# Products that nobody reads in TensorE's waits, and two modulation groups traced at another place

## The chip, the cores and the metric

The kernel runs on one core of a Trainium2 chip, in one launch. A core has five engines that run beside each other, each with its own queue in order: TensorE (PE in the profile; PEld is its weight load), VectorE (DVE), ScalarE (ACT), GpSimd (POOL) and SyncE (SP), which here only issues DMA transfers. ScalarE and GpSimd issue transfers too, from their own queues. TensorE writes to PSUM, eight banks of 128 x 512 f32. The metric is the device time of one execution in microseconds; lower is better.

## The reference, cut to what matters

The program is a hybrid layer on 256 tokens of 1024 channels, followed by a second block of two layers (differential and latent attention, a stick-breaking attention, two cross attentions, two MLPs), which the change does not touch. All data are f32. Of the first layer this matters here:

```python
mod = silu(c) @ ada_w + ada_b                    # 1024 x 6144
sh1, sc1, g1, sh2, sc2, g2 = split(mod, 6)
h = rms_norm(x, norm1_g) * (1 + sc1) + sh1       # first norm
z = h @ w_in                                     # q k v, index, rwkv (zr), two gates
attn = dsa_sparse_attention(...)                 # index scores, top 64, softmax
rw = rwkv7_branch(zr, ...)                       # a recurrence over the tokens
x = x + g1 * ((sigmoid(ga) * (attn @ w_attn_br) + sigmoid(gr) * (rw @ w_rwkv_br)) @ w_out)
h2 = rms_norm(x, norm2_g) * (1 + sc2) + sh2
x = x + g2 * moe_ffn(h2, ...)                    # router, top 8 of 64 experts, shared expert
```

The modulation has 6144 columns; the kernel makes them in three groups of 2048 (g = 0, 1, 2). Group 0 is sh1 and sc1, group 1 is g1 and sh2, group 2 is sc2 and g2. In `moe_ffn`, sigmoid scores choose 8 experts of 64 for each token, by groups; `sh_gate`, `sh_up` and `sh_down` are the shared expert, which all tokens use.

## The kernel before, in words

**Precision.** Most dense products are made of three products of split operands: `split_into` (L152, L153) writes a high part on ScalarE and the low rest on VectorE, and `mm3` (L186 to L188) adds high x high, high x low and low x high into one bank. Weights come in tiles of 128 x 2048 through SyncE's queue (`wload`, L142), from a ring of buffers, and are split in blocks of 1024 columns into three buffers. Transposes, the modulation and the experts' products are plain f32; a plain f32 product counts as two TensorE instructions in the trace.

**Order.** The program is traced in Python; a planner then sets the order of each engine's queue. An instruction that is traced earlier ranks higher; the planner goes through time by its own estimates of durations and gives each engine the highest-ranking instruction whose operands it holds to be there. So later work fills gaps of earlier work. On the chip each queue is strictly in that order: if an operand comes later than planned, the engine stands. `later(n)` lowers the rank of a block by n places. `after(engine)` sets what its block traces on that engine behind the last instruction traced there before; this is an order in the queue, not a wait.

**First norm.** `modulation(K, 0, ...)` (L965) multiplies the columns of silu(c) with eight blocks of ada_w, four products a block, into the bank "mod"; VectorE adds ada_b (L969). `first_h` meanwhile scales x and transposes it: `turn` (L1011) makes four transposes into a bank, three times ahead of the modulation's columns and once more behind them. `mod_cols` (L980) transposes the sum; from it come the scale s1 and the shift b1 (L1017, L1018). Then f = s * x + b (L1025, L1027) is split into hTh and hTl. `zr_in` makes the first projection products from it with `dense_T` (L186 to L188, tile hTh): a weight block of 1024 columns serves 24 products.

**Recurrence and modulation.** Behind `zr_in`, `first_mixer` traces modulation groups 1 and 2 and `router_in` with `later(400)`, behind ScalarE's last instruction at that place, and then `rwkv(K, zs, rwT, 0)`, the first half of the heads (four of eight). Each group has eight loads of 1 MB into one buffer "adaw" (SyncE's queue, L963), 32 products, a load of ada_b (ScalarE's queue, L952), the sum on VectorE (L969) and a store of the row to DRAM (ScalarE's queue, L972). The bank "mod" exists once, so group 2's first product needs group 1's sum to be done. `router_in` transposes the columns of groups 1 and 2, loads the router's weight and two small tensors on ScalarE's queue and one on GpSimd's, and makes eight products. The half of the recurrence is a chain of small products (L1082 to L1321) with VectorE and ScalarE between them; its last activation on ScalarE is the split of its result (L152, w<-rw). Behind it come the projections of the attention, the index scores and the choice (`dsa_choose`, L1367 to L1376, L1382), the second half of the recurrence, `dsa`, and the gates' projections.

**Routing.** `Moe.start` transposes the logits (L1655), finishes the shared expert's gate products, makes the row of norms (`row`, four products on TensorE at L295, a copy on VectorE at L298), and traces `hidden` (L1688 to L1693: copies, two products with the row on VectorE, a silu), `route` (VectorE, L1711 to L1752: sigmoid scores, the maxima by groups, the selection `selb` at L1737; three products with it on TensorE at L1741 to L1743; positions `pos` and gate weights `gw`) and `plan` (experts ordered by their number of tokens). `shared_in(K, "sh_up", up)` is a generator: the first `next` makes the products of the first half of the weight, the second those of the rest. `take` gathers the first experts' tokens: one-hot matrices P (L1873) and 32 products (L1887), which ScalarE and VectorE copy out of PSUM (L1894, L1892). The shared expert's down weight is split with the subtraction on GpSimd (L153 on POOL).

**Experts.** 64 experts in 26 units; each expert's three weights of 1 MB come through SyncE's queue (L1930, L1933) into the ring as buffers come free. The first ones are loaded ahead, until the ring is full.

## Time and profile before

| what | us |
|---|---|
| runs of the kernel before | 1696.97, 1698.87, 1699.32 |
| their median | 1698.87 |
| the profiled execution, its own time | 1700.63 |
| its span, first to last instruction | 1698.70 |
| TensorE busy | 1615.2 (95% of the span) |
| VectorE busy | 832.5 (49%) |
| ScalarE busy | 677.6 (40%) |
| GpSimd busy | 84.7 (5%) |
| mean granted clock of TensorE | 0.981 |

How the views are read. In the **stretches**, a line is a piece of time from the span's start: from:to and its length, then the busy time of PE, PEld, DVE, ACT and POOL, each with its count of instructions, then the mean granted clock of TensorE (1.00 is 2.4 GHz, 0.50 is 1.2 GHz), the busy share of the 16 DMA engines and GB/s. In the **timeline**, a line has the start, the length, the engine, the line of the kernel, the operation, out<-in by the program's names, the shape, and how many instructions were merged; in brackets stands how long the engine had been idle before, and what ended that. Successive products overlap, so the step from one start to the next is what a product costs, not its length. SPq and ACTq are the instructions that issue transfers. In the **list of transfers** a line has the count, the size of one and the median time from issue to landing; in the **view of one tile** a line has the shortest, median and longest duration in ns, and when the first and the last one began.

### The profile page before, as it was taken

What the parts mean: (1) busy time and instruction counts of PE and PEld (TensorE: products, weight loads), DVE (VectorE), ACT (ScalarE), POOL (GpSimd) and SP (SyncE); (2) the same over time, 40 slices, a digit from 0 to 9 for tenths busy, and PEclk for the clock granted to TensorE, in tenths of its full rate; (3) what the DMA queues carried; (4) which work ended last, traced back from release to release, by engine and by line L of the source; (5) the groups of instructions that cost most, each with busy time, mean ns of one, the idle gap of its engine ahead of it and who ended that gap; (6) DMA issues with size and microseconds to landing.
All of it is one profiled execution on the core that took longest, in us unless ns stands there. A gap on an engine that the chain in (4) does not pass through costs nothing. (4 is left out here: it accounts for less than half of the span.)

```text
span 1698.7 us, 28945 instructions
## 1 busy us (share of the span) xinstructions
PE 1615.2 (95%) x11894; PEld 1230.2 (72%) x11894; DVE 832.5 (49%) x1538; ACT 677.6 (40%) x1141; POOL 84.7 (5%) x105
## 2 busy tenths in 40 slices
PE   6999999997989999999999999999999999999997
PEld 3967667885547565546665587889998876989996
DVE  3664786676211311211211446666555677665554
ACT  3432444553122122122122546655444455554443
POOL 2000000103000000000000111211000000000000
PEclk8999899998999999999999999999999999999999
DMA  9555641874999999999999652546555533445551
GB/s 376 154 173 171 214 153 45 298 272 163 414 416 412 380 395 413 415 412 412 378 415 412 226 172 94 191 154 208 187 185 198 175 115 110 149 162 198 182 190 50
DMA packets 137942, 417.76 MB, mean 246 GB/s; under 512 B 10666, under 2 KB 17588, under 8 KB 118352
## 3 DMA queue, kind: packets, MB, share of 16 engines
q1 hardware_dynamic: 125872, 394.81, 62.3%
q0 software_dynamic: 4336, 12.34, 2.2%
q10 hardware_dynamic: 7600, 8.74, 1.8%
q8 instruction: 94, 1.54, 0.4%
q14 instruction: 40, 0.33, 0.1%
HBM read 409.57 MB, written 6.32 MB: 245 GB/s over the span
## 5 line engine op out<-in xcount | busy, mean ns | idle before, releaser
L153 DVE TENSOR_TENSOR w<-w 128x1024 fp32r<-128x1024 f32 (+1 forms) x283 | 347.6, 1230 | 259.0 <-ACT w L152 258.2
L152 ACT ACTIVATE w<-w 128x1024 fp32r<-128x1024 f32 (+1 forms) x285 | 299.9, 1054 | 317.6 <-PE acc L188 226.6
L1947 PE MATMUL tmp<-w 128*32 128x256 f32 (+2 forms) x2560 | 200.8, 393 | 10.2 <-DMA w<-in_exp_up_dram 8.6
L1947 PEld LDWEIGHTS tmp<-w 128*32 128x32 f32 (+2 forms) x2560 | 120.0, 121 | 81.9 <-issue 12.5
L188 PE MATMUL acc<-hTh,w 128*128 128x256 f32 (+2 forms) x552 | 159.0, 289 | 0.4 <-DVE w L153 0.4
L187 PE MATMUL acc<-hTl,w 128*128 128x256 f32 (+2 forms) x552 | 159.1, 288 | 0.0
L186 PE MATMUL acc<-hTh,w 128*128 128x256 f32 (+2 forms) x552 | 158.1, 287 | 0.7 <-ACT hTh L152 0.7
L186 PE MATMUL tmp<-hTh,w 128*128 128x256 f32 x512 | 143.3, 280 | 0.0
L188 PE MATMUL tmp<-hTh,w 128*128 128x256 f32 x512 | 142.9, 279 | 0.0
L187 PE MATMUL tmp<-hTl,w 128*128 128x256 f32 x512 | 142.9, 279 | 0.0
L188 PEld LDWEIGHTS acc<-hTh,w 128*128 128x128 f32 (+1 forms) x552 | 105.3, 191 | 5.5 <-issue 4.3
L187 PEld LDWEIGHTS acc<-hTl,w 128*128 128x128 f32 (+1 forms) x552 | 105.7, 192 | 4.3 <-issue 3.5
L1975 PE MATMUL tmp<-w,fT 128*32 128x512 f32 (+2 forms) x640 | 108.1, 598 | 0.5 <-ACT fT L1963 0.5
L186 PEld LDWEIGHTS acc<-hTh,w 128*128 128x128 f32 (+1 forms) x552 | 105.8, 192 | 3.3 <-issue 2.0
L186 PE MATMUL acc<-w,gh 128*128 128x512 f32 x256 | 99.9, 390 | 0.0
L188 PE MATMUL acc<-w,gl 128*128 128x512 f32 x256 | 99.8, 390 | 0.0
L187 PE MATMUL acc<-w,gh 128*128 128x512 f32 x256 | 99.7, 389 | 0.0
L186 PEld LDWEIGHTS tmp<-hTh,w 128*128 128x128 f32 x512 | 96.1, 188 | 0.5
L188 PEld LDWEIGHTS tmp<-hTh,w 128*128 128x128 f32 x512 | 96.2, 188 | 0.1
L187 PEld LDWEIGHTS tmp<-hTl,w 128*128 128x128 f32 x512 | 95.9, 187 | 0.5
L1951 ACT ACTIVATE fs<-tmp 128x256 f32<-128x256 f32 x26 | 10.0, 384 | 214.0 <-PE tmp L1947 214.0
L1953 DVE SCALAR_TENSOR_TENSOR ff<-tmp,gsl,fs 128x256 f32<-128x256 f32 x26 | 12.6, 484 | 167.4 <-ACT fs L1951 167.4
(633 smaller groups left out, 2913.0 us busy)
## 6 DMA issues: line engine op xcount, KB each, us to landing
w<-in_exp_gate_dram SPq DMA_DIRECT2D x64, 1024.0 KB, 15.7
w<-in_exp_up_dram SPq DMA_DIRECT2D x64, 1024.0 KB, 18.2
w<-in_exp_down_dram SPq DMA_DIRECT2D x64, 1024.0 KB, 14.8
w<-in_mlp_w_dram SPq DMA_DIRECT2D x64, 1024.0 KB, 5.2
w<-in_w_in_dram SPq DMA_DIRECT2D x23, 1024.0 KB, 6.0
adaw<-in_ada_w_dram SPq DMA_DIRECT2D x16, 1024.0 KB, 4.9
w<-in_xa_wkv_dram SPq DMA_DIRECT2D x16, 1024.0 KB, 12.7
w<-in_sb_w_in_dram SPq DMA_DIRECT2D x12, 1024.0 KB, 5.2
```

What stands on the lines that cost most here:

```text
L152: self.nc.scalar.activation(hi, src, AF.Copy)
L153: self.sub.tensor_tensor(lo, src, hi.bitcast(F32), op=OP.subtract)
L186: mm(out, lh, rh, start=first, stop=False, skip_group_check=True)
L187: mm(out, lh, rl, start=False, stop=False, skip_group_check=True)
L188: mm(out, ll, rh, start=False, stop=last, skip_group_check=True)
L1947: nc.tensor.matmul(b[at:at + w, x * 256:x * 256 + 256], X[:, k, i * 128 + at:i * 128 + at + w], d[n][:, k], start=(x == 0 and k == 0), sto ...
L1951: nc.scalar.activation(s, b[:, 0:256], AF.Silu)
L1953: nc.vector.scalar_tensor_tensor(f, b[:, 256:512], g, s, op0=OP.mult, op1=OP.mult)
L1975: nc.tensor.matmul(b[at:at + w], fT[:, k, at:at + w], d["exp_down"][:, k, n * 512:n * 512 + 512], start=(k == 0), stop=(k == 1), skip_grou ...
```

## The change

A new method `idle` makes n products of the identity with 512 columns of X (f32) into a bank that is not read, behind TensorE's last traced instruction. It is called three times: one product behind modulation group 0, three behind the last transposes of the first norm, five in `Moe.start`. There the second half of the sh_up products is traced directly behind the first, ahead of the five, of the row of norms and of `route`, and no longer behind `take`. In `first_mixer`, groups 1 and 2 and `router_in` are traced behind the first half of the recurrence, inside the scope "dsa", without `later(400)`; the block stands behind ScalarE's last instruction of the recurrence's half.

```diff
+    def idle(self, n, x, tag):
+
+        with self.after(self.PE):
+            b = self.bank(tag)
+            for _ in range(n):
+                self.nc.tensor.matmul(b, self.ident, x, start=True, stop=True, skip_group_check=True)
...
         if k < 7:
             yield
+    if g == 0:
+        K.idle(1, K.X[:, 0, :512], "acc")
     nc.vector.tensor_add(mb, b, mb)
...
             b = banks[k // 2] if k < 6 else turn(6, "tmp")
+            if k == 6:
+                K.idle(3, K.X[:, 0, :512], "acc")
             f = K.t([128, 2, T], "fhT", 2)
...
         adap = K.open("ada")
-        with K.later(400), K.after(K.ACT):
-            for g in (1, 2):
-                for _ in modulation(K, g, first, adap):
-                    pass
-            with K.stream(pool=first, tmp="mod"):
-                router_in(K, first)
         with K.scope("dsa"):
             with K.scope("rwkv0"):
                 rwkv(K, zs, rwT, 0)
+            with K.after(K.ACT):
+                for g in (1, 2):
+                    for _ in modulation(K, g, first, adap):
+                        pass
+                with K.stream(pool=first, tmp="mod"):
+                    router_in(K, first)
...
         rest = shared_in(K, "sh_up", up)
         next(rest)
+        next(rest, None)
+        K.idle(5, K.X[:, 0, :512], "mod")
         row = nm.row()
         s = K.t([128, 2, T], "shs")
         self.hidden(K.gate, s, row, True)
...
         self.take("S", {"S": 0}, tags=("tmp", "tmp", "acc"))
         next(plan, None)
-        next(rest, None)
         self.hidden(up, s, row, False)
```

## Rows read from the trace of the kernel before

**Rows 1.** Stretches: first projection, routing, experts; busy of five engines, clock, DMA.
```profile
42.50:85.00 42.50, 42.09 (x338) 38.81 (x337) 27.01 (x46) 20.57 (x30) 1.54 (x3) 1.00 0.50 154
...
395.00:405.00 10.00, 8.40 (x45) 7.05 (x44) 7.13 (x33) 4.30 (x7) 1.75 (x2) 0.61 0.00 1
...
600.00:700.00 100.00, 97.29 (x749) 59.29 (x748) 18.99 (x41) 23.89 (x43) 2.16 (x4) 1.00 1.00 405
```

**Rows 2.** Stretches between changes of the granted clock; its number is third from the end.
```profile
23.98:27.39 3.41, 2.81 (x29) 1.28 (x25) 0.00 (x0) 0.00 (x0) 0.00 (x0) 1.00 1.00 399
...
30.80:37.63 6.83, 5.84 (x25) 5.51 (x26) 6.71 (x10) 5.58 (x10) 3.01 (x6) 0.50 1.05 384
...
184.40:194.64 10.24, 8.07 (x33) 4.86 (x34) 4.79 (x12) 5.89 (x11) 0.00 (x0) 0.50 0.61 215
...
392.60:396.00 3.40, 0.40 (x6) 0.30 (x6) 3.12 (x22) 1.11 (x4) 0.00 (x0) 0.50 0.01 2
...
399.45:402.86 3.41, 3.37 (x16) 3.08 (x15) 1.18 (x10) 1.78 (x4) 0.00 (x0) 0.50 0.01 2
```

**Rows 3.** Timeline of TensorE at the first norm and the first projection products.
```profile
28.72 0.66 PE L980 MATMUL tmp<-ident,modr 128*128 128x128 f32 x4 [0.81 <-DVE modr L969]
29.80 0.63 PE L1011 MATMUL tmp<-ident,xs 128*128 128x128 f32 x4 [0.42 <-DVE b L1018]
...
32.08 0.80 PE L186 MATMUL acc<-hTh,w 128*128 128x256 f32 x2 [0.69 <-ACT hTh L152]
...
33.18 0.42 PE L188 MATMUL acc<-hTh,w 128*128 128x256 f32 x1
...
37.45 0.36 PE L188 MATMUL acc<-hTh,w 128*128 128x256 f32 x1
37.66 0.28 PE L186 MATMUL acc<-hTh,w 128*128 128x256 f32 x1
...
42.49 0.28 PE L188 MATMUL acc<-hTh,w 128*128 128x256 f32 x1
```

**Rows 4.** Timeline of VectorE there: low halves of the second and third weight block.
```profile
34.17 2.35 DVE L153 TENSOR_TENSOR w<-w 128x1024 fp32r<-128x1024 f32 x2
```

**Rows 5.** Timeline of TensorE in the experts: f32 products of 512 columns, 21 instructions.
```profile
653.26 9.28 PE L416 MATMUL tmp<-w,kvT 128*128 128x512 f32 x21 [1.35 <-ACT w L388]
```

**Rows 6.** Timeline of TensorE in the routing: first product with the selection, the gather.
```profile
395.60 0.21 PE L1741 MATMUL tmp<-selb,trib 128*128 128x64 bf16 x1 [5.38 <-DVE selb L1737]
...
397.40 0.58 PE L1887 MATMUL acc<-P,h2h 128*128 128x256 f32 x1 [0.15 <-DVE P L1873]
...
399.94 0.58 PE L1887 MATMUL tmp<-P,h2h 128*128 128x256 f32 x1
...
404.06 0.28 PE L1887 MATMUL tmp<-P,h2l 128*128 128x256 f32 x1
```

**Rows 7.** Timeline of VectorE in the routing, ahead of the selection.
```profile
391.82 0.40 DVE L298 COPY nrow<-tmp 128x256 f32<-128x256 f32 x1
...
392.33 0.76 DVE L1689 TENSOR_TENSOR shf<-rw,nrow 128x256 f32<-128x256 f32 x2
```

**Rows 8.** Timelines of GpSimd (the shared expert's split) and SyncE's queue (expert loads).
```profile
404.50 4.65 POOL L153 TENSOR_TENSOR w<-w 128x1024 fp32r<-128x1024 f32 x2
...
409.18 2.39 SPq L1933 DMA_DIRECT2D w<-in_exp_up_dram  x2
```

**Rows 9.** Modulation groups 1 and 2: tile view, TensorE, ScalarE, list of transfers.
```profile
L965 PE MATMUL mod<-adaw,c x128: 592/617/1061, 93.9 to 231.1; 128*32 128x512 f32 x128
...
172.77 1.06 PE L965 MATMUL mod<-adaw,c 128*32 128x512 f32 x8
...
188.43 1.93 PE L965 MATMUL mod<-adaw,c 128*32 128x512 f32 x8 [2.17 <-DMA adaw<-in_ada_w_dram]
...
175.24 0.60 ACT L152 ACTIVATE w<-rw 128x512 fp32r<-128x512 f32 x1 [1.89 <-PE rw L1321]
...
wr<-in_router_w_dram ACTq DMA_DIRECT2D x1, 256.0 KB, 6.3
```

## The prediction

> **What bounds the kernel now.** I read the stretches first (busy time of each engine, granted clock, DMA). TensorE is busy almost without a break in the first projection [rows 1], while its DMA is half idle: there TensorE's own work is the limit. From 395 to 405 us the DMA queues move 1 GB/s, and in the experts they are full, 405 GB/s [rows 1]. So the expert stage is a stream of weights whose length is fixed by bytes; what can be moved is the moment at which it starts again after the routing.
>
> Then the clock. It is granted in full (1.00, 2.4 GHz) from 23.98 to 27.39, while modulation products and transposes follow one another; it stands at 0.50 (1.2 GHz) from 30.80 to 37.63, from 184.40 to 194.64, and from 392.60 to 402.86 [rows 2]. Ahead of each fall TensorE waited: before 30.80 the modulation's sum and the columns had to pass through VectorE, before 392.60 the routing ran on VectorE for 5.38 us [rows 3, 6].
>
> The product rows show what the low level costs. At 0.50 one projection product follows the next after (37.45 - 33.18) / 20 = 0.213 us, at 1.00 after (42.49 - 37.66) / 41 = 0.118 us [rows 3]. The wait before 30.80 is thus paid a second time, by products that run at 1.2 GHz after it. The same holds for the gather of the first experts' tokens, at 397.40 to 404.18 [rows 6].
>
> **Part A, one and three unread products at the first norm.** One such product (128x512, f32) is two instructions. The nearest row of the same shape and type has 21 instructions in 9.28 us, 0.44 each, so 0.88 us a product at 2.4 GHz [rows 5]. The modulation's last product ended at 28.72 - 0.81 = 27.91 [rows 3]; the single product then ends at 28.79, and the column transposes start 0.07 us late. The three go behind the last four transposes of x, which end at 29.80 + 0.63 = 30.43 [rows 3], and end at 30.43 + 2.64 = 33.07. The first projection product started at 32.08 [rows 3]; it is now 0.99 us late, but at 2.4 GHz. By 37.63 the kernel before had made (37.63 - 32.08) / 0.213 = 26 products; now it is (37.63 - 33.07) / 0.118 = 38.6. The 12.6 more are worth 12.6 x 0.118 = 1.49 us. Is there work for them? The first 24 need one split weight block and last until 33.07 + 24 x 0.118 = 35.9; the low half of the second block is there after half of VectorE's 2.35 us, at 35.35 [rows 4]. So VectorE is no new limit. With the 0.07 us: **A = -1.4 us**. [...]
>
> **Part B, two modulation groups and the router's inputs traced behind the recurrence's first half.** What moves: 64 products, the 16 loads of ada_w on SP's queue (1 MB each, one buffer), two sums on VectorE, two loads of ada_b, two stores of the rows and the loads of the router on ScalarE's queue, one on GpSimd's, then the transposes and products of router_in. Before, they were ranked 400 places later than they stand, and their products ran from 93.9 to 231.1 [rows 9], spread over the recurrence: the 400 places had already put them behind most of it. Now they rank behind all of the half, and still above the projections that fill TensorE. SP's loads of ada_w still rank above the projections' weights, so SP's order changes little; GpSimd's load has no reader until the routing. By the code the rows and columns are first read for the output projection and the second norm, behind dsa and the gates, so nothing there is late.
>
> What does change is ScalarE's queue: ada_b of both groups now goes out behind the recurrence's last activation, which ends at 175.24 + 0.60 = 175.84 [rows 9]. A load of the same size on that queue landed after 6.3 us [rows 9]: 182.1. The sum of group 1 waits for it, and group 2's first product needs the bank of that sum. In the trace that product ran at 172.77 [rows 9]; it can't run before 182.1. If it keeps its place in TensorE's queue, everything behind it waits 182.1 - 172.8 = 9.3 us. On VectorE the sum stands in order too: the index scores queued behind it wait, and ScalarE's relu and TensorE's index products after them. If the planner, which orders queues by its own estimate, sets it behind other products, it costs nothing. On the other side, TensorE waited 2.17 us for an ada_w block just before 188.43 [rows 9], inside the stretch at 0.50 from 184.40, in which it was busy 8.07 us [rows 2]. If the new order takes away wait and low clock, that is up to 2.17 + 8.07 / 2 = 6.2 us. So B lies between -6.2 and +9.3 us. The row nearest to a wait that the planner misjudged is that 2.17 us, and one such wait can go as easily as one can come: **B = 0**.
>
> **Part C, the routing.** The second half of sh_up's products moves ahead in the program. They fill TensorE until 395.60 - 5.38 = 390.22 already [rows 6], so the move itself is worth nothing; what covers it is that they were ready by then. The five products follow them: 390.22 + 5 x 0.88 = 394.62. TensorE had to wait until 395.60 for the selection [rows 6], so they delay nothing, with 0.98 us to spare. The row of norms is now traced behind the five; its copy (0.40 us) and the two products with it (0.76 us) stood on VectorE ahead of the selection [rows 7] and slip behind it. The selection could be 1.16 us earlier; TensorE is free at 394.62 + 0.63 (the row's transposes, four like those of [rows 3]) = 395.25, so 0.35 us of it count (bounds 0 and 0.98).
>
> At 2.4 GHz the last 24 gather products take 24 x 0.118 = 2.83 us instead of 404.18 - 399.94 = 4.24 [rows 6]: 1.4 us. The first eight and the transposes of the gates between them took 399.94 - 397.40 = 2.54 us; TensorE's share of that halves, while copies on ScalarE stay: between 0 and 0.8 us, I take 0.6, since most of the 2.54 is TensorE's. Together 0.35 + 1.4 + 0.6: **C = -2.4 us**. It reaches the end because SP's first expert load after the routing, at 409.18, goes out when GpSimd's split ends at 404.50 + 4.65 = 409.15 [rows 8]; that split follows the gather's copies on ScalarE. From there the full DMA queues pass it on.
>
> **The sum.** A - 1.4, B 0, C - 2.4: -3.8 us. The profiled execution took 1700.63 us (span 1698.70), the runs' median is 1698.87, 1.76 us less. On the profiled execution the sum gives 1696.8; on the median **1695.1 us**, the forecast. Faster and slower mean by over 0.2%, 3.4 us, about what a measurement of this kernel can tell from no change; -3.8 lies just beyond.
>
> **The rivals.**
> - *The new wait* (slower). Group 2's first product keeps its place and TensorE stands behind ada_b until 182.1: +9.3 us, 1704.4. For it: TensorE's queue is in order, and it did stand behind ada_w [rows 9]. Against: the planner knows of the wait. It decides from 7.2 us on (3.8 + 3.4). Chance 0.13.
> - *The modulation's wait goes* (B at its good end): wait and low clock at 184 to 195 vanish, down to 1688.9, more likely half of it, 1692. For it: group 2's first block will have landed long before it is needed. Chance 0.19.
> - *The routing's clock falls anyway.* Behind the five products TensorE has only short work and waits until 397.40. The gather runs at 1.2 GHz as before; C is 0 or -0.35, the time some 1697.4. For it: in the stretch from 392.60 TensorE did 0.40 us of work and the clock stayed low until 402.86, with the gather under way [rows 2]. Chance 0.20.
> - [...] Chance 0.08, since in the stretch from 23.98 the clock stayed at 1.00 although transposes were among its work [rows 2]. [...]
> - The forecast, both clocks held and B within some 2 us: chance 0.40, its own range 1693 to 1697.5.
>
> **How the numbers follow.** The range leaves out the new wait (0.13) and the far end of the good case: 1690.0 to 1699.5. Faster: of the forecast's 0.40 a bit more than half, 0.24, of the good case 0.17, of the others 0.04, together 0.45. Slower: 0.11 of the new wait and 0.02 from the others, 0.13. Within 0.2%: the rest, 0.42.
>
> **What would show it.** A: granted clock 1.00 from 23.98 through the first projection, first product near 33.1, 0.118 us apart. B: ada_b's loads at 176 on ScalarE's queue, group 2 starting after 182, and no TensorE wait over 3 us there. C: the products end near 394.6, the gather's products 0.118 us apart, SP's first expert load 3 to 4 us earlier than 409.18 (A and C together). Wrong: a wait of TensorE for the sum on modr; clock 0.50 in the gather; an expert stage whose start moves but whose end doesn't.

## The result, and the profile after

| | kernel before | changed kernel |
|---|---|---|
| median, us (6 runs each, side by side) | 1700.3 | 1712.44 |
| lowest and highest, us | 1696.97 to 1706.77 | 1707.09 to 1718.06 |
| profiled execution, us | 1700.63 | 1711.12 |
| its span, us | 1698.70 | 1709.4 |

The ratio is 1.0074, with a 95% interval of 1.0054 to 1.0093: some 12 us slower, where 3.8 us faster was forecast. The two profiled executions differ by 10.7 us in span. Cut at four places of the program that both have, they differ like this (starts and ends in us, from the two traces):

| stretch | before | after | longer by |
|---|---|---|---|
| start to the first transpose of kw (behind the first projections) | 79.0 | 76.2 | -2.8 |
| from there to the transpose of the logits (recurrence, modulation, attention, second norm) | to 384.0 | to 390.9 | +9.7 |
| from there to the last product of the experts | to 951.6 | to 956.8 | -1.7 |
| from there to the end of the next layer's first products (L416 before, L423 after) | to 967.8 | to 978.9 | +5.9 |
| the rest | to 1698.7 | to 1709.4 | -0.4 |

The lines that answer to [rows 1, 2], stretches of the changed kernel with the clock third from the end:

```profile
30.80:37.63 6.83, 6.83 (x45) 5.47 (x45) 6.64 (x10) 6.42 (x11) 3.01 (x6) 1.00 1.05 387
90.19:100.43 10.24, 10.24 (x33) 6.08 (x33) 5.28 (x12) 1.49 (x4) 0.00 (x0) 0.50 0.18 50
178.86:182.35 3.49, 0.00 (x0) 0.00 (x0) 0.22 (x1) 0.00 (x0) 0.00 (x0) 1.00 1.00 227
182.35:189.17 6.82, 6.30 (x30) 4.41 (x32) 4.59 (x11) 3.63 (x6) 0.00 (x0) 0.50 0.66 230
395.00:405.00 10.00, 9.09 (x51) 5.93 (x50) 9.45 (x48) 2.35 (x4) 2.49 (x1) 1.00 0.05 20
960.58:967.40 6.82, 4.85 (x6) 2.18 (x7) 4.34 (x7) 3.26 (x6) 0.71 (x1) 0.50 1.03 374
```

The first line is what part A was to do: the same 6.83 us that stood at 0.50 before now stand at 1.00, and TensorE is busy in all of them. The fifth is part C: the routing at 1.00, where 0.61 was the mean before. The third is new: 3.49 us in which TensorE does nothing at all, and VectorE 0.22 us; the clock is at 1.00 there and at 0.50 in the 6.82 us behind it. The second line is longer than before: behind TensorE's wait for the first ada_w block of group 1 the clock stands at 0.50 for 10.24 us. In the kernel before it stood so for 3.41 us there:

```profile
99.07:102.48 3.41, 3.41 (x18) 3.38 (x16) 2.98 (x6) 2.24 (x3) 0.00 (x0) 0.50 0.02 7
```

**First norm.** TensorE's timeline, the answer to [rows 3]:

```profile
27.74 1.12 PE L137 MATMUL acc<-X,ident 128*128 128x512 f32 x2
28.70 0.60 PE L989 MATMUL tmp<-ident,modr 128*128 128x128 f32 x4
29.73 0.63 PE L1020 MATMUL tmp<-ident,xs 128*128 128x128 f32 x4 [0.42 <-DVE b L1027]
30.19 2.74 PE L137 MATMUL acc<-X,ident 128*128 128x512 f32 x6
32.37 0.80 PE L193 MATMUL acc<-hTh,w 128*128 128x256 f32 x2
...
33.49 0.28 PE L195 MATMUL acc<-hTh,w 128*128 128x256 f32 x1
...
37.60 0.28 PE L195 MATMUL acc<-hTh,w 128*128 128x256 f32 x1
```

The unread products (L137) stand where the waits of [rows 3] were. From 33.49 to 37.60 lie 35 steps of 0.117 us, against 0.213 before.

**Modulation.** Timelines of ScalarE's queue, VectorE and TensorE around the sum of group 1, the answer to [rows 9]:

```profile
174.68 1.19 ACTq L959 DMA_DIRECT2D modr<-in_ada_b_dram  x2
175.91 0.48 ACTq L1553 DMA_DIRECT2D wr<-in_router_w_dram  x1
176.43 6.03 ACTq L1556 DMA_DIRECT2D iot<-in_c_part_dram  x1
182.85 0.54 ACTq L981 DMA_DIRECT2D modrow<-modr  x1
183.92 0.44 ACTq L1367 DMA_DIRECT2D cau<-in_c_causal_dram  x1
...
182.13 0.69 DVE L978 TENSOR_TENSOR modr<-mod,modr 128x512 f32<-128x512 f32 x1 [5.53 <-DMA modr<-in_ada_b_dram]
...
182.87 1.93 PE L972 MATMUL mod<-adaw,c 128*32 128x512 f32 x8 [4.01 <-DVE modr L978]
```

ada_b goes out at 174.68; VectorE's sum waits 5.53 us for it; TensorE waits 4.01 us for the sum; the store of the row (modrow) is issued when the sum is there, and the loads behind it on ScalarE's queue, cau with the causal mask for the index scores among them, go out after it. Three queues stand in order behind one transfer.

**Routing.** Timelines of TensorE, VectorE, ScalarE, GpSimd and SyncE's queue, the answers to [rows 6 to 8]:

```profile
396.54 4.45 PE L137 MATMUL mod<-X,ident 128*128 128x512 f32 x10
400.83 0.61 PE L302 MATMUL tmp<-ident,nrs 128*128 128x128 f32 x4
401.28 0.19 PE L1753 MATMUL tmp<-selb,trib 128*128 128x64 bf16 x1
403.64 0.28 PE L1899 MATMUL acc<-P,h2l 128*128 128x256 f32 x1
403.75 0.28 PE L1899 MATMUL acc<-P,h2h 128*128 128x256 f32 x1
...
401.48 0.42 DVE L305 COPY nrow<-tmp 128x256 f32<-128x256 f32 x1
...
403.01 1.28 ACT L1703 ACT_TABLE_LOAD   x1
404.31 0.91 ACT L1703 ACTIVATE shs<-shf,shb 128x256 f32<-128x256 f32 x2
408.22 0.63 ACT L159 ACTIVATE w<-shs 128x512 fp32r<-128x512 f32 x1 [1.67 <-DVE shs L1705]
...
410.16 4.84 POOL L160 TENSOR_TENSOR w<-w 128x1024 fp32r<-128x1024 f32 x2
...
415.03 1.16 SPq L1945 DMA_DIRECT2D w<-in_exp_up_dram  x2
```

The five products end at 400.99 and the gather's products now follow each other after 0.12 us. But the row of norms (nrs, nrow) comes behind the five, so the gate's silu with its table load lies between 403 and 405, behind the selection; before, it stood ahead of it. The split of shs waits for it, then GpSimd's split, then SyncE's first expert load. That load comes 415.03 - 390.89 = 24.1 us behind the logits' transpose; in the kernel before it was 409.18 - 383.95 = 25.2 us. TensorE's part got faster, the chain that ends at SyncE hardly. The transposes, of the kernel before and of the changed kernel:

```profile
383.95 0.33 PE L1655 MATMUL tmp<-ident,lgT 64*128 64x64 f32 x2 [0.95 <-ACT lgT L1652]
390.89 0.33 PE L1666 MATMUL tmp<-ident,lgT 64*128 64x64 f32 x2 [0.97 <-ACT lgT L1663]
```

**The end of the experts' loop.** TensorE waits 5.72 us there, 2.17 us before, for the same product. TensorE's waits of the changed kernel and of the kernel before (us in total, times, longest):

```profile
PE tmp L423 <- DMA w<-in_ev_w_in_dram: 5.7, 1, 5.7
PE tmp L416 <- ACT w L388: 2.2, 1, 2.2
```

The view names a load for the longer wait. But in both kernels the product starts 0.06 us behind the end of TensorE's third branch at the loop (962.49 and 962.55, 953.73 and 953.79), so it is the branches that hold it. The view of the loop's line (For_i, L2059 before and L2071 after) has the branches of each queue, here TensorE's; minimum, median and maximum in ns. Of the changed kernel:

```profile
L2071 PEldq COMPARE_BRANCH  x3: 101/193/3851, 956.7 to 962.3; - x3
```

and of the kernel before:

```profile
L2059 PEldq COMPARE_BRANCH  x3: 97/187/315, 951.5 to 953.5; - x3
```

One of the three branches takes 3.85 us in place of 0.32 us. It jumps over the body of the loop that this input does not run. DMA in those 3.85 us (957.05 to 960.90), by queue, with packets, MB and share:

```profile
q1 hardware_dynamic: 361, 0.74, 61.3%
q8 instruction: 1, 0.02, 2.4%
```

One packet of instructions arrives in it. In the kernel before no packet falls into the branch. Nothing of this was in the forecast.

### The profile page after: what moved, and what is told of

Same layout as the page of the kernel before. It is cut to its first block, busy times and chain, and to the rows that moved or that the text cites. A ratio compares the mean times of both kernels' runs of the same rounds, so it can differ in the third digit from the quotient of the medians.

```text
span 1709.4 us, 28983 instructions
## 1 busy us (share of the span) xinstructions
PE 1630.8 (95%) x11912; PEld 1235.5 (72%) x11912; DVE 833.9 (49%) x1538; ACT 681.0 (40%) x1143; POOL 84.6 (5%) x105
## 3 DMA queue, kind: packets, MB, share of 16 engines
q8 instruction: 94, 1.54, 0.4%
## 5 line engine op out<-in xcount | busy, mean ns | idle before, releaser
L1959 PEld LDWEIGHTS tmp<-w 128*32 128x32 f32 (+2 forms) x2560 | 119.9, 120 | 81.4 <-DMA w<-in_exp_up_dram 10.8
L1965 DVE SCALAR_TENSOR_TENSOR ff<-tmp,gsl,fs 128x256 f32<-128x256 f32 x26 | 12.6, 483 | 163.7 <-ACT fs L1963 163.7
```

What stands on the lines that cost most here:

```text
L1959: nc.tensor.matmul(b[at:at + w, x * 256:x * 256 + 256], X[:, k, i * 128 + at:i * 128 + at + w], d[n][:, k], start=(x == 0 and k == 0), sto ...
L1965: nc.vector.scalar_tensor_tensor(f, b[:, 256:512], g, s, op0=OP.mult, op1=OP.mult)
```

## The experiments

Eighteen kernels, each timed against the kernel before on the same chip: 12 runs of each, 29 to 35 of the kernel before (the first row is from the runs above). Ratios are given with their 95% intervals; 0.001 is 1.7 us. The last columns come from each kernel's profile: TensorE's longest wait for modr, the branch at the loop's end, and the time from the logits' transpose to the experts' last product.

| run | ratio | interval | modr, us | branch, us | routing and experts, us |
|---|---|---|---|---|---|
| changed kernel | 1.0074 | 1.0054 to 1.0093 | 4.0 | 3.85 | 565.9 |
| norm_routing | 1.0038 | 1.0021 to 1.0055 | 0 | 3.34 | 567.8 |
| move_only | 1.0032 | 1.0011 to 1.0053 | 4.8 | 0.32 | 564.8 |
| early_bias | 1.0038 | 1.0020 to 1.0056 | 0 | 3.58 | 566.9 |
| routing_only | 1.0033 | 1.0011 to 1.0054 | 0 | 3.60 | 569.3 |
| before_padded | 1.0023 | 1.0005 to 1.0040 | 0 | 3.37 | 565.2 |
| after_short | 1.0035 | 1.0017 to 1.0053 | 5.3 | 0.40 | 568.9 |
| row_first | 1.0020 | 1.0005 to 1.0036 | 0 | 0.40 | 573.3 |
| norm_padded | 1.0011 | 0.9990 to 1.0032 | 0 | 0.42 | 565.4 |
| early_short | 1.0014 | 0.9997 to 1.0032 | 0 | 0.40 | 567.8 |
| no_edge_short | 1.0024 | 1.0007 to 1.0042 | 0 | 0.40 | 569.3 |
| routing_short | 1.0029 | 1.0010 to 1.0049 | 0 | 0.42 | 569.4 |
| before_tiny | 1.0007 | 0.9989 to 1.0025 | 0 | 0.42 | 563.0 |
| routing_low | 1.0022 | 1.0005 to 1.0040 | 0 | 0.42 | 569.1 |
| norm_routing_low | 1.0018 | 0.9999 to 1.0036 | 0 | 0.40 | 571.4 |
| mended | 1.0035 | 1.0013 to 1.0057 | 0 | 0.40 | 569.0 |
| late_row | 1.0019 | 1.0003 to 1.0034 | 0 | 0.32 | 568.4 |
| fill_row | 1.0025 | 1.0009 to 1.0042 | 0 | 0.40 | 568.7 |
| norm_fill | 1.0010 | 0.9992 to 1.0027 | 0 | 0.40 | 568.3 |

An interval is some 3 us wide to either side, so a single pair settles little under 4 us. The columns from the profiles show where time goes, but each is of one execution, and the runs of one kernel differ by up to 16 us; the profiles of norm_routing, row_first and norm_routing_low are of the longest of their twelve runs. Where columns and ratios agree I take it as shown.

### Apart: the moved groups and the unread products

**norm_routing** puts the moved block back to its old place.

```diff
+        with K.later(400), K.after(K.ACT):
+            for g in (1, 2):
...
         with K.scope("dsa"):
             with K.scope("rwkv0"):
                 rwkv(K, zs, rwT, 0)
-            with K.after(K.ACT):
-                for g in (1, 2):
...
```

> The unread products and the earlier second half of sh_up, with the two modulation groups left where they were. Theory 1 (the moved groups cost the time: group 1's sum stands behind ada_b): TensorE reaches the first product on adaw 3.8 us earlier than before, as in the changed kernel, keeps that to 205 us, the routing gives 1 to 4 us more: 3 to 7 us faster than before, no TensorE wait over 3 us between 170 and 205. Rival (the unread products themselves cost it): as slow as the changed kernel, +8 us or more. Rival on the loop's end (TensorE's branch there takes 3.85 us instead of 0.32 because of where the code lies, not because of a part of the change): the branch may be long or short here whatever the rest does; if long, the gain is 3.5 to 6 us smaller.

Measured: +6.5 us. The wait for modr is gone, but the gain isn't there, and the branch is long; theory 1 allowed for +3 us at most with a long branch.

**move_only** is the kernel before with that block moved, and nothing else.

```diff
-        with K.later(400), K.after(K.ACT):
...
+            with K.after(K.ACT):
+                for g in (1, 2):
...
```

> Only the two modulation groups and router_in are moved; no unread products, sh_up as before. Theory 1: the wait for modr near 179 to 183 is there, the index products end some 12 to 15 us later than in the kernel before less what the clock gives back, the end is 7 to 13 us later than before (some 6 of them only if the branch at the loop's end is long). Rival (unread products cost it): within 2 us of before.

Measured: +5.4 us; the wait for modr is there (4.8 us), the branch is short. The two kernels' excesses, 6.5 and 5.4 us, add up to 11.9, and the changed kernel has 12.6: the two halves of the change each cost about half.

**early_bias** traces the two loads of ada_b where they stood, and keeps the rest of the block moved.

```diff
+        with K.later(400), K.after(K.ACT):
+            for g in (1, 2):
+                bias(K, g, first)
         with K.scope("dsa"):
...
```

> The changed kernel, but the two loads of ada_b are traced where they stood before (ahead of the recurrence, behind ScalarE's last instruction there, 400 places later); everything else of the two groups stays moved. Theory 1: TensorE's 4.0 us wait for modr at 179 to 183 goes, with it the low clock at 182 to 189, and ScalarE's loads behind the row's store go out 4 to 7 us earlier; 5 to 10 us faster than the changed kernel, so -4 to +4 us against before. Rival (the place of the 64 products and their weight loads costs it, whatever ada_b does): the wait goes, but another TensorE wait or low clock takes its place between 170 and 205, and the time stays within 3 us of the changed kernel's.

Measured: 1.0038, which is 6 us less than the changed kernel, with no wait of TensorE for modr. It is still 6.5 us over the kernel before, where +4 was the theory's upper end. The queues' order is another one, too: the recurrence's last activation ends at 183.5 us instead of 175.3, and ScalarE's loads behind the row's store go out no earlier (cau at 185.13, 183.92 in the changed kernel), where 4 to 7 us earlier was expected.

**routing_only** leaves only the routing's part.

```diff
-    if g == 0:
-        K.idle(1, K.X[:, 0, :512], "acc")
...
-            if k == 6:
-                K.idle(3, K.X[:, 0, :512], "acc")
...
```

> Only the routing's part: sh_up's second half earlier and the five unread products. In the changed kernel TensorE's first expert product came 4.0 us earlier against the stretch before the routing, SyncE's first expert load only about 1 us. Theory 1 (the end follows SyncE's first expert load): 0.5 to 2 us faster than before. Rival (the end follows TensorE's first expert product, as forecast with -2.4): 2.4 to 4 us faster. If the branch at the loop's end is long here, 3.5 to 6 us are to be added to either.

Measured: +5.6 us, with a long branch. Behind the logits' transpose it took 569.3 us to the experts' end, 1.6 more than the profiled execution of the kernel before and 4.1 more than the mean of the five kernels that have the routing as it was or with tiny products (565.2, below). Neither theory had the routing itself longer.

### The branch

All four kernels with unread products had a long branch, move_only had not. A product of f32 is two weight loads and two products in the trace (18 and 18 at L137 for the changed kernel's nine), so the nine make TensorE's program 36 instructions longer ahead of the loop.

**before_padded** adds 20 instructions to the kernel before and next to no work.

```diff
+        K.idle(5, K.X[:, 0, :2], "mod")
         with K.after(PE):
             self.route(lg, rs)
```

> The kernel before, with five unread products of two columns each in TensorE's 5.4 us wait of the routing: 20 instructions more ahead of the experts' loop (each f32 product is two weight loads and two products), next to no time. Theory (the length of TensorE's code ahead of the loop's end decides whether the branch there stands for code that is still to be loaded): the branch takes 3 to 4 us instead of 0.32, the clock stands at 0.50 behind it, the second block starts 5 to 6 us later: 1.0025 to 1.004 of before. Rival (the branch is long because of what the unread products or the moved groups do to transfers or time): branch 0.32 us, no change.

**after_short** makes the changed kernel's program longer still, by 36 instructions.

```diff
-        K.idle(5, K.X[:, 0, :512], "mod")
+        K.idle(14, K.X[:, 0, :128], "mod")
```

> The changed kernel with 14 unread products of 128 columns in the routing in place of five of 512: about the same time on TensorE, 36 instructions more ahead of the loop, 71 more than the kernel before. Code is loaded in pieces of 16 KB, and the branch of the changed kernel comes just behind such a load; 36 instructions, some 4 us of experts' work, later the piece should be there. Theory (code length): branch 0.3 us again, the time 5 to 6 us under the changed kernel's, 1.003 to 1.005 of before; the wait for modr near 179 to 183 stays. Rival (long because of the changed kernel's transfers): branch stays above 3 us, time as the changed kernel's.

Measured: both branches as the theory of code length had it; the ratios are 1.0023, just under its range, and 1.0035, inside. TensorE's branches in before_padded:

```profile
L2068 PEldq COMPARE_BRANCH  x3: 97/193/3371, 948.6 to 953.6; - x3
```

and in after_short:

```profile
L2071 PEldq COMPARE_BRANCH  x3: 97/187/398, 955.7 to 957.8; - x3
```

The packets of instructions on queue q8 are of 16 KB (94 with 1.54 MB in the kernel before). In the kernel before, the next packet comes at 952.88, when the branch (0.32 us from 951.84) is through. With 20 to 36 instructions more the packet falls into the branch (958.00 in the changed kernel, 0.95 us behind the start of the branch at 957.05 and not just ahead of it, as the expectation of after_short had it). With 56 or more it comes ahead of it, in after_short at 950.17, 5.8 us before the branch. The twenty profiles fall into these three groups without exception: a packet 0.95 to 1.03 us into the long branch in five, 1.04 to 1.05 us behind the start of a short one in the three kernels of unchanged length, 5.2 to 6.2 us ahead of a short one in the other twelve. Why the branch is long when a packet comes in it, and what the packets hold, no trace shows. In all five kernels with a long branch the stretch from the experts' last product to the end of the next layer's first products is 21.7 to 22.2 us, in all others 16.1 to 18.0: 4 to 6 us, the branch's 3 to 3.5 and the low clock behind it. The ratios say the same less sharply: 6.6 us between the changed kernel and after_short, 4.1 between early_bias and early_short, 2.7 between before_padded and before_tiny, 0.7 between routing_only and routing_short.

### The wait for ada_b again, with the branch short

**early_short** is after_short with the loads of ada_b early (the edit of early_bias).

> The run with 14 short products (branch at the loop's end short again, 1.0035 of before), and in addition the two loads of ada_b traced where they stood before, as in the run early_bias. Theory (the wait for ada_b is the larger part of what the moved groups cost, 4 of some 6 us): no TensorE wait for modr near 180, 3 to 6 us faster than the run with 14 short products, 0.999 to 1.0015 of before. Rival (the place of the groups costs it whatever ada_b does): 1.0025 to 1.004 of before.

**no_edge_short** is after_short without the order edge.

```diff
-            with K.after(K.ACT):
-                for g in (1, 2):
...
+            for g in (1, 2):
+                for _ in modulation(K, g, first, adap):
+                    pass
```

> The run with 14 short products, without the order edge behind ScalarE's last instruction: the groups stay traced behind the recurrence's half, but ScalarE may issue their loads whenever the planner finds it free, which it does at the start of the program. Theory (the edge is what makes ada_b late): as the run early_short, 0.998 to 1.0015 of before. Rival (the rank of the groups costs it, or the two early loads of 256 KB delay the first norm): 1.0025 or more, the first norm later than 76 us at the products of kw.

Measured: early_short 1.0014, 3.6 us less than after_short and no wait for modr. The intervals overlap; the profiles agree with the sign, 308.2 us from kw to the logits' transpose against 310.7. TensorE's waits between 90 and 206 us (us in total, times, longest) are then for ada_w alone:

```profile
PE mod L981 <- DMA adaw<-in_ada_w_dram: 4.9, 2, 4.4
```

no_edge_short has no wait for modr either, but now the loads of ada_b and of the router go out in the first microseconds, and the first norm pays: kw's transposes start at 85.6 instead of 76.2. From there to the logits it makes up all of it (300.5 us instead of 310.7), and 1.0024 is on the rival's side. So the edge is not needed to move the groups, and without it the loads go too early.

### The routing

**row_first** takes the moved block back, has the 14 short products, and traces the row and the gate's silu ahead of sh_up's second half.

```diff
         next(rest)
-        next(rest, None)
-        K.idle(5, K.X[:, 0, :512], "mod")
         row = nm.row()
         s = K.t([128, 2, T], "shs")
         self.hidden(K.gate, s, row, True)
+        next(rest, None)
+        K.idle(14, K.X[:, 0, :128], "mod")
```

> Both sets of unread products, the modulation groups left where they were, 14 products of 128 columns in the routing (branch as in the run before this one), and the row of norms and the gate's silu traced ahead of sh_up's second half and of the unread products. Theory (in the changed kernel the row slipped behind the five products, so that the silu with its 1.28 us table load fell between the gather's copies and the splits of the shared expert, and SyncE's first expert load came no earlier): the table load is back ahead of the selection, GpSimd's split starts right behind the gather, SyncE's first expert load comes 2 to 4 us earlier against the logits' transpose than in the kernel before; 3 to 5 us faster than before, 0.997 to 0.9985. Rival (the split waits for something else): SyncE's load no earlier, only the first norm's 1 to 2 us are gained.

Measured: SyncE's first expert load came 408.72 - 387.55 = 21.2 us behind the logits' transpose, as expected, but the time, 1.0020, was no better for it. In the profile, which is of the longest of the twelve runs, the experts ended 573.3 us behind the transpose, the latest of all. GpSimd's split now ran beside VectorE's work on the order of the experts, and two small instructions of that took over 2 us each (VectorE's timeline):

```profile
404.24 2.15 DVE L2059 TENSOR_SCALAR lit<-io 1x16 f32<-1x16 f32 x1
...
406.54 2.17 DVE L1800 SCALAR_TENSOR_TENSOR rank<-rs,rank 64x1 f32<-64x1 f32 x1
```

so TensorE's first expert product came at 414.34, 26.8 us behind the transpose, against 23.6 in the kernel before. The stream of loads started earlier and was not used in that execution.

**routing_short** is routing_only with the 14 short products, and **before_tiny** the kernel before with 14 products of two columns ahead of `route`; both have a short branch.

> Only the routing's part, with 14 short products in place of five, so that the branch at the loop's end is short. Theory (the routing's unread products hold the clock in the gather, but the row's slip puts the silu and its table load behind the selection, so SyncE's first expert load gains nothing): 0.999 to 1.0008 of before, SyncE's first expert load 25 to 26 us behind the logits' transpose, as in the run with the routing's part alone. Rival (the part gains its 2.4 us, and only the branch hid that): 0.9978 to 0.999.

> The kernel before with 14 unread products of two columns in the routing's wait: 56 instructions more, the branch short. In the run with five of them the routing was 4.2 us shorter, of which 3 us by VectorE's sum with the bias, which stood 1.5 us behind GpSimd's subtraction there and 4.5 us in the kernel before. Theory (that was the draw of the execution): within 0.1% of before, 0.9985 to 1.001. Rival (the products themselves shorten the routing): 0.9965 to 0.998.

Measured: routing_short 1.0029, worse than either theory had it; before_tiny 1.0007, not to be told from no change, as its theory had it. With the branch out of the way, the routing's part costs time by itself. VectorE's timelines told where to look: where GpSimd makes its two subtractions of the second norm (h2l, 6.7 us there), one VectorE instruction stands. In before_tiny:

```profile
386.41 0.24 DVE L1790 TENSOR_SCALAR low<-io,iot 64x64 f32<-64x64 f32 x1
...
389.42 1.46 DVE L1723 TENSOR_TENSOR ch<-sc,rbias 128x128 f32<-128x128 f32 x1 [1.26 <-ACT sc L1722]
```

The comparison into low takes 0.24 us, ahead of GpSimd's; the sum with the bias takes 1.46 where 0.27 is its shortest time (in the changed kernel). With the routing's part the planner sets the comparison behind the logits, into VectorE's wait for the sigmoid, and there it stands until GpSimd is done with its first or its second instruction (2.7 us in the changed kernel, 5.7 in most others).

**routing_low** traces the comparison ahead of the second norm's rows; **norm_routing_low** adds the first norm's products; **mended** is the whole change with the loads of ada_b early, the short products and this edit.

```diff
         K.open("route", "right", cur=True)
+        self.low = K.t([64, 128], "low")
+        K.nc.vector.tensor_scalar(self.low[:, :64], self.io[:64, :64], K.iot[:64], None, op0=OP.is_lt)
...
-        ts(low, self.io[:64, :64], iot, None, op0=OP.is_lt)
```

> The routing's part with 14 short products (1.0029 of before), and the comparison into low traced ahead of the second norm's rows, so that VectorE makes it before GpSimd's subtraction begins. Theory (the loss is that comparison, which the planner puts into VectorE's wait and which then stands behind GpSimd with the selection behind it): nothing but the sum with the bias stands, 1.4 to 1.5 us; TensorE's first product with the selection 9.0 to 9.4 us behind the logits' transpose instead of 10.6; 1.5 to 4 us faster than the run without this edit, 1.0005 to 1.002 of before. Rival (the silu and its table load behind the selection are the loss): the selection comes earlier, SyncE's first expert load stays 25 us or more behind the logits' transpose, 1.0025 or more.

> The same with the unread products of the first norm. If the first norm's 2 us at 78 us reach the end: 0.9985 to 1.001 of before, 1 to 2 us below the run routing_low. If they are lost at the waits behind it: as routing_low.

> All of the change with three mends: ada_b loaded where it was, 14 short products in the routing (short branch), the comparison into low ahead of GpSimd's subtraction. Theory (wait for ada_b, branch and comparison are the three losses): 8 to 13 us faster than the changed kernel, 0.998 to 1.001 of before. Rival (moving the groups costs something of its own): 1.002 or more.

Measured: the theory fell. The comparison is out of the way, and two other instructions stand in its place (VectorE of routing_low):

```profile
385.55 2.94 DVE L1585 TENSOR_TENSOR w<-w,b 128x1024 f32<-128x1024 f32 x1
...
391.03 3.02 DVE L1724 TENSOR_TENSOR ch<-sc,rbias 128x128 f32<-128x128 f32 x1 [1.02 <-ACT sc L1723]
```

The selection comes no earlier (397.9 - 387.1 = 10.8 us behind the transpose; 10.6 without the edit), and the ratios stay: 1.0022, and 1.0018 for norm_routing_low, not to be told from each other. mended, which was to repair all three losses, is at 1.0035, on the side of its rival that moving the groups costs something of its own. That rival stays open: early_short, which differs from mended by the comparison's place alone, was at 1.0014, and TensorE's waits for ada_w between 90 and 206 us are 4.9 us there and 8.0 us in mended's profile.

**late_row** makes only the move of sh_up's second half; **fill_row** adds only 14 products of 128 columns ahead of `route`; **norm_fill** adds the first norm's products to that.

```diff
         next(rest)
+        next(rest, None)
         row = nm.row()
...
         next(plan, None)
-        next(rest, None)
```

> The kernel before, with sh_up's second half traced ahead of the row of norms and of the gate's silu, as in the change, and no unread product anywhere; TensorE's code is as long as before, so the branch at the loop's end is short. Theory (the move makes the row late, and the row's copy, the silu and its table load come behind the selection): SyncE's first expert load 25 to 28 us behind the logits' transpose, 1.001 to 1.003 of before. Rival (the unread products cost it): 21 to 23 us, 0.999 to 1.001.

> The kernel before, with 14 unread products of 128 columns behind the row of norms, everything else in its place; branch short. Theory (the products hold the clock in the gather and cost nothing): SyncE's first expert load 20.5 to 22 us behind the logits' transpose, gather products 0.12 us apart, 0.998 to 1.0005 of before. Rival (the products push TensorE's other work behind the selection): 24 us or more, 1.001 or more.

> The same with the unread products of the first norm, so both clocks are held and nothing else is changed. Theory (the first norm's 2 us reach the end): 0.9965 to 0.9995 of before. Rival (they are lost at the waits for adaw at 90 to 102 us): as the run fill_row.

Measured: late_row, without any unread product, has the routing of the changed kernel: the comparison, the table load and SyncE's load (timelines of VectorE, ScalarE and SyncE's queue),

```profile
384.78 5.72 DVE L1781 TENSOR_SCALAR low<-io,iot 64x64 f32<-64x64 f32 x1
390.43 0.28 DVE L1714 TENSOR_TENSOR ch<-sc,rbias 128x128 f32<-128x128 f32 x1
...
396.68 1.28 ACT L1691 ACT_TABLE_LOAD   x1
...
410.86 0.81 SPq L1933 DMA_DIRECT2D w<-in_exp_up_dram  x2
```

410.86 - 383.99 = 26.9 us behind the transpose, and 1.0019, both within what its theory said. So the reordering, which the forecast counted at nothing, costs time by itself. fill_row isn't free either (1.0025, its rival's side; SyncE's load at 23.1 us, between the two): the products go ahead of sh_up's second half on TensorE, part of which then lies behind the selection. Which of the two costs more, the ratios don't tell. norm_fill is at 1.0010, over its theory's 0.9995 and under fill_row. norm_padded, which has only the first norm's products, and ten products of two columns in the routing to keep the branch short, was expected 0.5 to 2.5 us faster than the kernel before; it is at 1.0011, with no change inside its interval. In time from the transpose to the experts' end: 563.0 to 567.7 us (mean 565.2) in the five kernels whose routing is untouched or has products of two columns, 568.3 to 568.7 in these three, 565.9 to 573.3 in the twelve with the change's own order or mends of it.

No version beat the kernel before.

## Why the prediction was wrong

**Part A: the mechanism was right up to 79 us, and its size larger than forecast; that it reaches the end is not shown.** The clock holds through the transposes and the first projection: 1.00 from 27.39 to 37.63, with 0.117 us a product. A fall of the clock there, to which the forecast gave 0.08, is not in the trace: the transposes, from 28.70 to 30.36, stood between unread products, and the clock stayed. The first product came at 32.37 and not at 33.07, since it starts beside the end of the three. Ten profiles with these products start kw's transposes at 76.1 to 77.5 (mean 76.4; no_edge_short is left out), nine without at 77.9 to 79.2 (mean 78.6): 2.1 us, where -1.4 stood. Behind that the gain can't be followed in the ratios: norm_padded and norm_fill, at 1.0011 and 1.0010, are not faster than the kernel before, but their intervals reach down to 0.9990 and 0.9992, which would leave room for the 1.4 us. The profiles point to what took it back. From kw to the logits' transpose, with the groups unmoved, five profiles with the products take 305.0 to 312.9 us (mean 310.2), eight without 304.5 to 309.2 (mean 306.7). The time goes with the clock: three of the thirteen with 13.7 us at 0.50 in that piece take 304.5 to 304.9 us, the two with 30.7 us 312.6 and 312.9; norm_padded, 305.0 with 20.5 us, is the one that falls out. The part that differs most lies behind the wait for the first ada_w block of group 1, where the clock stands at 0.50 for 13.7 us in four of the five with the products, and for 3.4 to 10.2 us in seven of the eight without. In norm_routing:

```profile
91.52:105.17 13.65, 12.79 (x52) 10.06 (x53) 5.42 (x12) 3.56 (x5) 0.00 (x0) 0.50 0.25 80
```

So the forecast followed the clock up to 37.63 us and put nothing in the sum for the wait behind it, which TensorE now reaches some 2 us earlier. That the earlier arrival is what lengthens the low stretch is argued, not shown: before_tiny has 13.7 us there without the products.

**Part B: the step that failed is "B = 0".** "The planner knows of the wait" was the reason given; it kept group 2's first product in its place all the same. The rival of the new wait had the place, the cause and the end of the wait (182.1 forecast, 182.13 for the sum and 182.87 for TensorE in the trace), and a chance of 0.13. That 182.1 and 182.13 agree so closely is luck: the recurrence's last activation ended 0.6 us earlier than before, at 175.27, and ada_b took longer than the 6.3 us. Its price was 9.3 us for the wait alone; measured are 4.0 to 5.3 us of wait, since TensorE had projections to do until 178.86, and a low clock behind it (0.50 from 182.35 to 189.17), and in runs 5.4 us for the move alone. Loading ada_b early gives back 6.1 us (changed kernel to early_bias, clear of the noise) and 3.6 us (after_short to early_short, not clear of it); what the moved groups cost beyond that stays open. B's good end rested on a wrong reading: in the 7 us ahead of the fall at 184.40 TensorE waited 0.40 us at most, and the 2.17 us wait ended at 188.43, behind the fall, so the low clock was not that wait's price. What argued for the rival stood in the forecast already: the engines take their queues in order, ada_b could not go out before the recurrence's last activation, and its transfer takes 6.3 us [rows 9]. The stall needed no misjudgement of the planner by any odd amount; an edge placed by hand made the load late for every order that keeps the product where it was.

**Part C: the step that failed is "the move itself is worth nothing", and with it the row that "slips behind".** The forecast saw that the row's copy and its two products would slip behind the selection, and counted it as a gain of 0.35 us. It did not follow the row to its reader: the silu with its 1.28 us table load, the split of shs on ScalarE, GpSimd's split, and SyncE's load, the very chain that it named as the end of the part. The clock did hold in the gather (-1.4 us of the sum, right), and the chain to SyncE ran past it. The second error is one of reading: 25.2 us from the logits' transpose to SyncE's load was the longest of the five profiles that have the routing untouched or with tiny products (20.8 to 22.7 in the others), because the sum with the bias stood 4.5 us behind GpSimd in that one execution and 1.4 to 1.5 in the others. In the kernel before:

```profile
386.28 4.47 DVE L1714 TENSOR_TENSOR ch<-sc,rbias 128x128 f32<-128x128 f32 x1 [1.28 <-ACT sc L1713]
```

So the 5.38 us wait into which the five products were to fit was a draw as well: in move_only, whose routing is the same, TensorE waits 2.87 us for the selection, less than the 4.4 us of the five. And what looked like a gain of 1.7 us in the changed kernel's profile is none against the mean of 565.2.

**Not in the sum at all: the branch.** Every instruction of an unread product was costed as time on TensorE, and none as a place in its program. By the three groups of profiles, the 36 instructions made a branch long that comes more than 500 us later: 3.85 us in place of 0.32, then 6.82 us at a clock of 0.50, 5.9 us in the profile.

The stretches together: -2.8 + 9.7 - 1.7 + 5.9 - 0.4 = +10.7 us, the difference of the spans. They are not the parts: the 9.7 us hold B's wait, and also the 6.8 us that the clock stood longer at 0.50 near 90 to 106 us, some 3.4 us by an estimate at half speed. The forecast's own list of what would prove it wrong had two of the three signs, a wait of TensorE for the sum on modr, and an expert stage whose start moves but whose end doesn't.

## What to carry to other kernels

When a load is tied behind an instruction by hand, cost the stall as certain, from the end of that instruction plus the transfer, unless the work that needs it is seen to move; an order that a planner chooses does not mend an edge that it was given. A clock that is held over one wait can be lost at the next (here 1.00 from 30.80 to 37.63, and 0.50 from 90.19 to 100.43), so follow it past the stretch that was mended. When a step slips, follow it to its last reader, through table loads and splits, before calling the slip a gain. And added instructions are also added code: with a jump in the program, a few dozen of them, though they cost no engine any time where they stand, can decide whether the jump takes 0.3 or 3.4 us and more; pad or shorten the program on purpose when two versions are compared.

## What was not expected of the hardware

- The same branch of TensorE took 0.32 to 0.42 us or 3.34 to 3.85 us, by the length of the code ahead of it alone: +0 instructions short, +20 to +36 long, +56 and more short.
- A comparison of 64 x 64 took 0.24 us alone and 5.72 us beside GpSimd's subtractions, and a sum of 128 x 128 between 0.27 and 4.47 us. GpSimd's two subtractions take 6.7 to 6.9 us either way; it is VectorE that stands. With the two back to back, VectorE sometimes gets through between them (1.46 us; in the changed kernel the comparison takes 2.72 us and ends at 394.40, GpSimd's first subtraction at 394.34) and sometimes only behind the second (5.72 us; in the kernel before the sum takes 4.47 us and ends at 390.75, GpSimd's second at 390.59). Why VectorE stands no run shows.
- The clock stood at 1.00 through all 3.49 us in which TensorE did nothing (178.86 to 182.35) and at 0.50 in the 6.82 us of work behind it: the price of this wait came after it.
- One issue on ScalarE's queue (iot, 176.43) is shown with 6.03 us, and the store that needs the sum is issued right behind it (182.85): the transfers behind a waiting store waited too. The same issue is shown with 6.73 us in move_only and 7.22 us in after_short, which have the wait, and with 0.58 us in early_bias; why it is long no run shows.
